# The rotary part of an attention's scores taken over 128 instead of 64 partitions

## The chip, the cores and the metric

The kernel runs on one core of a Trainium2 chip. The metric is the device time of one execution in microseconds (us). Five engines matter: TensorE (PE; its weight loads are listed apart as PEld), VectorE (DVE), ScalarE (ACT), GpSimd (POOL) and the queue of SyncE (SP), which issues the loads of weights.

## The reference, cut to what matters

One block of an encoder: a retention branch and a latent attention branch, merged by gates, then an MLP. The change lies in the attention, 16 heads over 256 tokens. Each head's score has two parts, one over 128 channels of its own and one over 64 rotary channels whose key is the same for all heads:

```python
q_nope, q_pe = q[..., :QK_NOPE], _rope(q[..., QK_NOPE:], positions)      # 128 and 64 wide
k_pe = _rope(k_pe.reshape(B, S, 1, QK_ROPE), positions)                  # one for all heads
qf = jnp.concatenate([q_nope, q_pe], axis=-1)
kf = jnp.concatenate([k_nope, jnp.broadcast_to(k_pe, (B, S, MLA_HEADS, QK_ROPE))], axis=-1)
s = jnp.einsum('bqhd,bkhd->bhqk', qi, k) * scale     # masked by chunks, then softmax, then values
```

## The kernel before

All weights are float32 in memory. A weight tile `raw` is loaded by SP, rounded into `hi` by ACT, and the remainder `lo` is made by DVE; a product of two such pairs takes three matmuls (hi*hi, hi*lo, lo*hi), which the helper `mm3` (lines 585 to 589) writes out. The first 128 queries of a head instead go through one plain float32 matmul, recorded by the profile as two passes (16 heads give 32 records).

The attention is written group by group, four heads to a group: `mla_projections` makes the group's queries, keys and values (tiles `lt`, then `q0`, `qs`, `k0`, `ks`; values in `v`), while `mla_attention` of the group before runs between its steps: `mla_scores`, `mla_turn` (transposes into `mt`), `mla_values` (into `my`). The last group runs between the first products of the output matrix (`mo`). This part has no order written out by hand: a scheduler lays the instructions out for each engine when the program is built, from its own estimates, so an edit moves instructions beyond those that it names. The stages before (`gm` and earlier) and the MLP behind have an order written by hand.

In `mla_scores`, a head h takes eight matmul instructions into one PSUM tile `ms`: line 1014 (own channels, plain float32), line 1015 (rotary channels, plain float32), then `mm3` over the own channels and `mm3` over the rotary channels. The rotary queries of two heads lie on top of each other in one tile of 128 partitions (`pe`, and split in `vkp`), even heads on partitions 0 to 63 and odd heads on 64 to 127; the rotary key `kpe` lies there twice, once in each half. A rotary product of a head therefore takes the slice `b` of 64 partitions. The split rotary key is `kps`, a quarter-thousand columns twice in slot 4 of the big tile `vkp` (line 1006), made once by ACT (line 554) and DVE (line 555).

Of the kernel before, what the change touches and what calls it, by code (L numbers as in the profile page):

```python
# [12 lines left out]
F32 = mybir.dt.float32  # L13
# [6 lines left out]
P = 128  # L20
S = 256
# [84 lines left out]
def block_kernel(ctx: ExitStack, tc: tile.TileContext, A):  # L106
    nc = tc.nc
    V, SC, G, PE = nc.vector, nc.scalar, nc.gpsimd, nc.tensor
# [7 lines left out]
    def big(name, dt=F32, shape=(P, KT, S)):  # L116
        return act.tile(list(shape), dt, tag="act16", name=name)
# [31 lines left out]
    def mmps(name):  # L149
        return pmm.tile([P, 512], F32, tag="mm", name=name)  # L150

    def atps(name):
        return pat.tile([P, 512], F32, tag="at", name=name)
# [40 lines left out]
    def lora_pair(src, x, whole=False):  # L194
        hi, lo = weights(src, [P, 2, LT, P])
        ps = mmps(f"lt{uid[0]}")
        for i in range(2):
            out = ps[:, i * S : (i + 1) * S]
            for k in range(LT):
                PE.matmul(out, hi[:, i, k], x.hi(k), start=k == 0, stop=False)  # L200
                PE.matmul(out, hi[:, i, k], x.lo(k), start=False, stop=False)
            for k in range(LT):
                PE.matmul(out, lo[:, i, k], x.hi(k), start=False, stop=k == LT - 1)
            yield i, out if not whole else ps

    def n_unit(outs, src, x, k0, nk, start, stop):
        for kh in range(0, nk, 2):
            w = weights(src[:, kh : kh + 2], [P, 2, 512])
            first, last = start and kh == 0, stop and kh == nk - 2
            for t, out in enumerate(outs):  # L210
                n_tile(out, w, x, t, k0 + kh, 2, first, last)
# [340 lines left out]
    def split(hi, lo, val, scale=None):  # L552
        if scale is None:
            SC.copy(hi, val)  # L554
            V.tensor_tensor(out=lo, in0=val, in1=hi.bitcast(F32), op=ALU.subtract)  # L555
        else:
            SC.activation(hi, val, AF.Copy, scale=scale)
            V.scalar_tensor_tensor(
                lo, in0=val, scalar=scale, in1=hi.bitcast(F32), op0=ALU.mult, op1=ALU.subtract
            )  # L560
# [24 lines left out]
    def mm3(out, st, mv, start=True, stop=True):  # L585
        (sh, sl), (mh, ml) = st, mv
        PE.matmul(out, sh, mh, start=start, stop=False)
        PE.matmul(out, sh, ml, start=False, stop=False)
        PE.matmul(out, sl, mh, start=False, stop=stop)
# [99 lines left out]
    def rope(out, ps, cos, sin, step):  # L689
        n = ps.shape[1]  # L690
        tmp = rope_pool.tile([P, n, S], F32, tag="rope", bufs=1, name="rope")
        cos, sin = (t.rearrange("p (o n) -> p o n", o=1) for t in (cos, sin))
        for d in range(0, P, step):
            s = d + step if (d // step) % 2 == 0 else d - step
            V.tensor_tensor(
                out=tmp[d : d + step],
                in0=ps[s : s + step],
                in1=sin[s : s + step].to_broadcast([step, n, S]),
                op=ALU.mult,
            )  # L700
        V.tensor_tensor(out=out, in0=ps, in1=cos.to_broadcast([P, n, S]), op=ALU.mult)
        V.tensor_tensor(out=out, in0=out, in1=tmp, op=ALU.add)
# [210 lines left out]
    with ExitStack() as mctx:  # L913
        cc = big("cc", F32R, shape=(P, 2 * LT, 2, S))
        kpe = rope_pool.tile([P, S], F32, tag="kpe", bufs=1, name="kpe")
# [84 lines left out]
        mp = mctx.enter_context(tc.tile_pool(name="mp", bufs=1))  # L1000
# [2 lines left out]
        heads, probs, outs = {}, {}, {}  # L1003

        vkp = big("vkp", F32R, (P, 8, 512))
        kps = vkp[:, 4].rearrange("p (j n) -> p j n", j=2)
        split(kps[:, 0], kps[:, 1], kpe)

        def mla_scores(h):
            q0, qs, k0, ks = heads.pop(h)  # L1010
            pe0, ps = heads[h // 2, "pe"]
            b = slice(64 * (h % 2), 64 * (h % 2) + 64)
            pS = atps(f"ms{h}")
            PE.matmul(pS[:, :P], q0, k0, start=True, stop=False)
            PE.matmul(pS[:, :P], pe0[b, :P], kpe[b, :P], start=False, stop=True)
            mm3(pS[:, P:384], (qs[:, 0], qs[:, 1]), (ks[:, 0], ks[:, 1]), stop=False)
            mm3(pS[:, P:384], (ps[b, 0], ps[b, 1]), (kps[b, 0], kps[b, 1]), start=False)
            pr = mp.tile([P, 384], F32, tag="pr", bufs=3, name=f"pr{h}")
            mx = mp.tile([P, 32], F32, tag="mx", bufs=4, name=f"mx{h}")[:, :4]
            parts = (slice(0, P), slice(P, 384))  # L1020
            for j, sl in enumerate(parts):
                V.tensor_tensor_reduce(
                    pr[:, sl], pS[:, sl], mask[:, sl], QK_SCALE, LOWEST, ALU.add, ALU.max, mx[:, j : j + 1]
                )
            V.tensor_scalar(mx[:, :2], mx[:, :2], -1.0, None, op0=ALU.mult)
            for j, sl in enumerate(parts):
                SC.activation(
                    pr[:, sl], pr[:, sl], AF.Exp, bias=mx[:, j : j + 1],
                    accum_out=mx[:, 2 + j : 3 + j],
                )  # L1030
            V.reciprocal(mx[:, 2:], mx[:, 2:])
            for j, sl in enumerate(parts):
                SC.activation(pr[:, sl], pr[:, sl], AF.Copy, scale=mx[:, 2 + j : 3 + j])
            probs[h] = pr
# [30 lines left out]
        def mla_projections(g):  # L1065
            j0 = 2 * (g % 2)
            for i, ps in lora_pair(A["w_qpe"][g // 2, :, j0 : j0 + 2], cq, True):
                if i:
                    pe = mp.tile([P, 2, S], F32, tag="pe", bufs=2, name=f"pe{g}")
                    rope(pe, ps.rearrange("p (i n) -> p i n", i=2), *tabs[1], 32)  # L1070
                    pes = vkp[:, 5 + g % 2].rearrange("p (i j n) -> p i j n", i=2, j=2)
                    split(pes[:, :, 0], pes[:, :, 1], pe[:, :, P:])
                    for n in range(2):
                        heads[2 * g + n, "pe"] = pe[:, n], pes[:, n]
                yield
            for jj in range(2):
                js = slice(2 * jj, 2 * jj + 2)
                qh = []
                for i, ps in lora_pair(A["w_qn"][g, :, js], cq):
                    h = 4 * g + 2 * jj + i  # L1080
                    q0 = mp.tile([P, P], F32, tag="q0", bufs=6, name=f"q0{h}")
                    qs = mp.tile([P, 2, P], F32R, tag="qs", bufs=6, name=f"qs{h}")
                    SC.copy(q0, ps[:, :P])
                    split(qs[:, 0], qs[:, 1], ps[:, P:])
                    qh.append((q0, qs))
                    yield
                for i, ps in lora_pair(A["w_kn"][g, :, js], ckv):
                    h = 4 * g + 2 * jj + i
                    k0 = mp.tile([P, P], F32, tag="k0", bufs=6, name=f"k0{h}")
                    ks = mp.tile([P, 2, S], F32R, tag="ks", bufs=6, name=f"ks{h}")  # L1090
                    SC.copy(k0, ps[:, :P])
                    split(ks[:, 0], ks[:, 1], ps)
                    heads[h] = (*qh[i], k0, ks)
                    yield
            pss = [mmps(f"v{g}{t}") for t in range(2)]
            for kh in range(2):
                n_unit(pss, A["w_v"][g, :, 2 * kh : 2 * kh + 2], ckv, 2 * kh, 2, kh == 0, kh == 1)
                yield
            vs = vkp[:, 2 * (g % 2) : 2 * (g % 2) + 2]
            split(vs[:, 0], vs[:, 1], pss[0])  # L1100
            v1 = mp.tile([P, 512], F32, tag="v1", bufs=2, name=f"v1{g}")
            SC.copy(v1, pss[1])
            heads[g, "v"] = vs, v1
# [19 lines left out]
        def mla_attention(g):  # L1123
            plan = {}
            slots = SLOTS[g == 3]
            for fn, when in zip((mla_scores, mla_turn, mla_values), slots):
                for i in range(4):
                    plan.setdefault(when[i], []).append((fn, 4 * g + i))
            for slot in range(max(plan) + 1):
                for fn, h in plan.get(slot, ()):  # L1130
                    fn(h)
                yield
# [7 lines left out]
        for g in range(4):  # L1140
            interleave(mla_projections(g), mla_attention(g - 1) if g else iter(()))
# [438 lines left out]
```

## Time and profile before

| | |
|---|---|
| time, median of 3 runs | 1575.42 us (1575.08 to 1575.52) |
| time of the profiled execution | 1575.46 us |
| span of its instructions | 1573.7 us |
| PE busy | 1562.7 us (99%) |
| DVE busy | 1332.8 us (85%) |
| ACT busy | 957.4 us (61%) |
| POOL busy | 36.7 us (2%) |
| granted TensorE clock, mean | 0.998 |

The profiled execution lies within the spread of the timed runs. The 1.8 us between its time and its span lie outside the instructions. The busy time of PE is modelled, and matmuls overlap: a record of 0.28 us can be followed by the next 0.12 us later. The pace is therefore read from the chain of waits, whose pieces do not overlap.

### The profile page before, as it was taken

How to read it: one execution, taken by the hardware profiler on the slowest of the kernel's cores; microseconds unless marked ns; L12 is line 12 of the kernel's file. 1: busy time of each engine (PE TensorE's matmuls, PEld its weight loads, DVE VectorE, ACT ScalarE, POOL GpSimd, SP SyncE). 2: the span in 40 equal slices, each digit the busy share in tenths (PEclk: the TensorE clock that was granted, in tenths of full speed). 3: DMA queues.
4: the chain of work that ended last, by engine and by line, in shares of the span. 5: the costliest groups of instructions: out<-in, count | busy, mean ns of one | idle time of the engine just before them, and what ended most of it. 6: DMA issues, size and time to landing. Idle time of an engine off the chain costs nothing.

```text
span 1573.7 us, 21491 instructions
## 1 busy us (share of the span) xinstructions
PE 1562.7 (99%) x7759; PEld 1319.5 (84%) x7759; DVE 1332.8 (85%) x1775; ACT 957.4 (61%) x1397; POOL 36.7 (2%) x71
## 2 busy tenths in 40 slices
PE   9999999999999999999999999999999999999997
PEld 7888888888898889888888888888888888888886
DVE  7898877899977986764667798999999899979996
ACT  6645655566545656664445576767677766655664
POOL 0000000000000000000000000000000100000000
PEclk9999999999999999999999999999999999999999
DMA  9666655466656563334565676667666977767773
GB/s 321 203 206 205 231 167 162 152 204 207 203 174 225 200 201 135 129 126 147 188 227 175 216 249 213 225 220 228 224 224 210 376 261 244 242 243 255 259 262 116
DMA packets 106986, 332.66 MB, mean 211 GB/s; under 512 B 11136, under 2 KB 12032, under 8 KB 105856
## 3 DMA queue, kind: packets, MB, share of 16 engines
q1 hardware_dynamic: 103632, 317.66, 60.1%
q0 software_dynamic: 3104, 11.54, 1.8%
q10 hardware_dynamic: 144, 2.10, 0.4%
q8 instruction: 61, 1.00, 0.3%
q14 instruction: 45, 0.37, 0.1%
HBM read 318.67 MB, written 12.58 MB: 210 GB/s over the span
## 4 chain that ended last, share of the span: by engine, by line
PE 77%; DVE 3%; issue 1%; ACT 1%; DVEq 0%; POOLq 0%; POOL 0%; ACTq 0%
PE dn L362 7%; PE dn L363 7%; PE dn L361 7%; PE z L176 6%; PE z L180 3%; PE zs L338 3%; PE zs L339 3%; PE zs L337 3%; PE mo L216 2%; PE mo L219 2%; PE mo L217 2%; PE wo L219 2%; PE wo L216 2%; PE wo L217 2%; PE gm L363 2%; PE gm L361 2%
## 5 line engine op out<-in xcount | busy, mean ns | idle before, releaser
L555 DVE TENSOR_TENSOR lo<-raw,hi 128x1024 fp32r<-128x1024 f32 (+3 forms) x238 | 254.4, 1085 | 26.8 <-ACT hi L554 26.4
L554 ACT CAST hi<-raw 128x1024 fp32r<-128x1024 f32 (+3 forms) x238 | 219.2, 940 | 59.1 <-PE yr L363 7.5
L169 DVE TENSOR_TENSOR lo<-raw,hi 128x1024 fp32r<-128x1024 f32 (+1 forms) x148 | 173.3, 1172 | 95.0 <-ACT hi L168 94.8
L168 ACT CAST hi<-raw 128x1024 fp32r<-128x1024 f32 (+1 forms) x148 | 149.5, 1011 | 160.0 <-PE mo L217 47.2
L554 ACT CAST hi<-forms 128x1024 fp32r<-128x1024 f32 x57 | 60.1, 1054 | 75.0 <-DVE forms L311 33.2
L555 DVE TENSOR_TENSOR morelo<-raw,morehi 128x1024 fp32r<-128x1024 f32 (+1 forms) x86 | 91.5, 1084 | 4.0 <-ACT morehi L554 3.9
L361 PE MATMUL dn<-hi,dd 128*128 128x512 f32 x240 | 93.5, 389 | 0.0
L363 PE MATMUL dn<-hi,dd 128*128 128x512 f32 x240 | 93.4, 389 | 0.0
L362 PE MATMUL dn<-lo,dd 128*128 128x512 f32 x240 | 93.4, 389 | 0.0
L554 ACT CAST morehi<-forms 128x1024 fp32r<-128x1024 f32 x51 | 53.8, 1054 | 58.5 <-DVE forms L321 32.1
L554 ACT CAST morehi<-raw 128x1024 fp32r<-128x1024 f32 (+1 forms) x86 | 78.9, 939 | 4.6 <-PE dn L363 2.8
L176 PE MATMUL z<-hT,hi 128*128 128x512 f32 x304 | 75.9, 392 | 0.0
L555 DVE TENSOR_TENSOR lo<-forms,hi 128x1024 fp32r<-128x1024 f32 x57 | 69.6, 1222 | 1.6 <-ACT hi L554 0.4
L311 DVE TENSOR_TENSOR forms<-raw,sraw 128x1024 f32<-128x1024 f32 x54 | 65.9, 1220 | 0.0
L176 PEld LDWEIGHTS z<-hT,hi 128*128 128x128 f32 x304 | 55.7, 188 | 10.7
L555 DVE TENSOR_TENSOR morelo<-forms,morehi 128x1024 fp32r<-128x1024 f32 x51 | 62.3, 1222 | 0.9
L361 PE MATMUL dn<-morehi,dd 128*128 128x512 f32 x146 | 56.8, 389 | 0.0
L362 PE MATMUL dn<-morelo,dd 128*128 128x512 f32 x146 | 56.8, 389 | 0.0
L363 PE MATMUL dn<-morehi,dd 128*128 128x512 f32 x146 | 56.8, 389 | 0.0
L362 PEld LDWEIGHTS dn<-lo,dd 128*128 128x128 f32 x240 | 45.1, 188 | 9.4
L361 PEld LDWEIGHTS dn<-hi,dd 128*128 128x128 f32 x240 | 45.1, 188 | 9.4
L363 PEld LDWEIGHTS dn<-hi,dd 128*128 128x128 f32 x240 | 45.1, 188 | 9.3
(512 smaller groups left out, 4371.2 us busy)
## 6 DMA issues: line engine op xcount, KB each, us to landing
raw<-w_down SPq DMA_DIRECT2D x106, 512.0 KB, 6.0
raw<-w_up SPq DMA_DIRECT2D x64, 512.0 KB, 4.6
raw<-w_rv SPq DMA_DIRECT2D x32, 512.0 KB, 4.6
raw<-w_rg SPq DMA_DIRECT2D x32, 512.0 KB, 4.1
raw<-w_gret SPq DMA_DIRECT2D x32, 512.0 KB, 4.2
raw<-w_ret_o SPq DMA_DIRECT2D x32, 512.0 KB, 4.8
raw<-w_gmla SPq DMA_DIRECT2D x32, 512.0 KB, 4.2
raw<-w_mla_o SPq DMA_DIRECT2D x32, 512.0 KB, 3.5
```

The costliest lines, as they stand in the source:

```text
L168: SC.copy(hi, raw)
L169: V.tensor_tensor(out=lo, in0=raw, in1=hi.bitcast(F32), op=ALU.subtract)
L176: PE.matmul(out, w[0][:, k], x.both(k0 + k), start=start and k == 0, stop=False)
L216: PE.matmul(out, x.hi(k0 + k, ts), w[0][:, k], start=start and k == 0, stop=False)
L217: PE.matmul(out, x.lo(k0 + k, ts), w[0][:, k], start=False, stop=False)
L219: PE.matmul(out, x.hi(k0 + k, ts), w[1][:, k], start=False, stop=stop and k == nk - 1)
L311: V.tensor_tensor(out=self.fa, in0=self.rb[:, 1:].to_broadcast([P, 2, 512]), in1=self.ra, op=ALU.add)
L361: PE.matmul(q, ah, wh, start=start, stop=False)
L362: PE.matmul(q, ah, wl, start=False, stop=False)
L363: PE.matmul(q, al, wh, start=False, stop=self.left[f] == 0)
L554: SC.copy(hi, val)
L555: V.tensor_tensor(out=lo, in0=val, in1=hi.bitcast(F32), op=ALU.subtract)
```

## The change

The rotary key gets a tile `kz` of 128 partitions with two copies: in copy 0 the key stands on partitions 0 to 63 and zeros on the rest, in copy 1 the other way round. POOL clears `kz`, ACT copies `kpe` into its two halves, and the split (ACT and DVE) is now made of `kz`, so it has 512 columns instead of 256 and takes slots 4 and 5 of `vkp`; the split queries move to slots 6 and 7. Each rotary product takes all 128 partitions: the query tile holds two heads, and the zeros of the key's copy remove the other one.

```diff
+        kz = mp.tile([P, 2, S], F32, name="kz")
+        G.memset(kz, 0.0)
+        for i in range(2):
+            b = slice(64 * i, 64 * i + 64)
+            SC.copy(kz[b, i], kpe[b])
-        kps = vkp[:, 4].rearrange("p (j n) -> p j n", j=2)
-        split(kps[:, 0], kps[:, 1], kpe)
+        kps = vkp[:, 4:6].rearrange("p j (i n) -> p j i n", i=2)
+        split(kps[:, 0], kps[:, 1], kz)
...
-            PE.matmul(pS[:, :P], pe0[b, :P], kpe[b, :P], start=False, stop=True)
+            PE.matmul(pS[:, :P], pe0[:, :P], kz[:, i, :P], start=False, stop=True)
...
-            mm3(pS[:, P:384], (ps[b, 0], ps[b, 1]), (kps[b, 0], kps[b, 1]), start=False)
+            mm3(pS[:, P:384], (ps[:, 0], ps[:, 1]), (kps[:, 0, i], kps[:, 1, i]), start=False)
...
-                    pes = vkp[:, 5 + g % 2].rearrange("p (i j n) -> p i j n", i=2, j=2)
+                    pes = vkp[:, 6 + g % 2].rearrange("p (i j n) -> p i j n", i=2, j=2)
```

The number and the columns of the matmuls stay. The scheduler places them anew from head 1 on. Behind line 1007 the line numbers of the changed kernel are 5 higher than those of the kernel before. On PE, around the scores of head 7 (`ms7`), with the transposes of head 4 (`mt4`) and projections of the next group (`lt`) beside them, the kernel before has:

```order
L1040 MATMUL mt4_6027<-con_105,pr4_5892 128x128
L1014 MATMUL ms7_6077<-k07_5797,q07_5741 128x128
L1015 MATMUL ms7_6077<-kpe_4028,pe1_5533 128x128
L1040 MATMUL mt4_6027<-con_105,pr4_5892 128x128 x2
L587 MATMUL ms7_6077<-ks7_5798,qs7_5742 128x256
...
L587 MATMUL ms7_6077<-vkp_5231 128x256
L588 MATMUL ms7_6077<-vkp_5231 128x256
...
L589 MATMUL ms7_6077<-vkp_5231 128x256
```

and the changed kernel, from the float32 product of the rotary channels on:

```order
L1020 MATMUL ms7_6081<-kz_5232,pe1_5537 128x128
...
L587 MATMUL ms7_6081<-ks7_5802,qs7_5746 128x256
L588 MATMUL ms7_6081<-ks7_5802,qs7_5746 128x256
L589 MATMUL ms7_6081<-ks7_5802,qs7_5746 128x256
L587 MATMUL ms7_6081<-vkp_5231 128x256
L588 MATMUL ms7_6081<-vkp_5231 128x256
L589 MATMUL ms7_6081<-vkp_5231 128x256
```

What stood between the rows of head 7's `mm3` over the rotary channels now stands ahead of them. On ACT, at the start of the attention, where the first projections are rounded and copied out (`hi641` is the last weight tile that it rounds ahead of them, `q00` and `k00` belong to head 0), the kernel before has:

```order
L168 CAST hi641_5401<-raw640_5400 128x1024
L1083 COPY q00_5296<-lt633_5283 128x128
L554 CAST qs0_5297<-lt633_5283 128x128
L1091 COPY k00_5337<-lt636_5324 128x128
L554 CAST ks0_5338<-lt636_5324 128x256
L554 CAST vkp_5231<-pe0_5267 128x2x128
L168 CAST hi644_5444<-raw643_5443 128x1024
```

and the changed kernel:

```order
L168 CAST hi641_5405<-raw640_5404 128x1024
L1010 COPY kz_5232<-kpe_4028 64x256 x2
L1088 COPY q00_5300<-lt633_5287 128x128
L554 CAST qs0_5301<-lt633_5287 128x128
L554 CAST vkp_5231<-kz_5232 128x512
L1096 COPY k00_5341<-lt636_5328 128x128
L554 CAST ks0_5342<-lt636_5328 128x256
L554 CAST vkp_5231<-pe0_5271 128x2x128
L168 CAST hi644_5448<-raw643_5447 128x1024
```

Three instructions of ACT have come between; the split of `kpe` has left its old place in the gate stage before. DVE makes the remainder of the split at the same place of its own order:

```order
L555 TENSOR_TENSOR qs0_5301<-lt633_5287,qs0_5301 128x128
L555 TENSOR_TENSOR vkp_5231<-kz_5232,vkp_5231 128x512
L555 TENSOR_TENSOR ks0_5342<-lt636_5328,ks0_5342 128x256
L702 TENSOR_TENSOR pe0_5271<-pe0_5271,rope_5272 128x512
L555 TENSOR_TENSOR vkp_5231<-pe0_5271,vkp_5231 128x2x128
L169 TENSOR_TENSOR lo645_5449<-raw643_5447,hi644_5448 128x1024
L555 TENSOR_TENSOR qs1_5318<-lt633_5287,qs1_5318 128x128
```

In the kernel before the same rows stand without the second. POOL has one new instruction, the clearing, which waits for the last gated output `gm` of the stage before (line 738), since `kz` lies in memory that this stage used. SP's order is the same in both kernels.

## Rows read from the trace of the kernel before

**Rows 1.** Busy us and count by engine in three stretches.

```profile
core 0: us, PE busy (x) PEld busy (x) DVE busy (x) ACT busy (x) POOL busy (x), PEclk, DMA share, GB/s
595.00:700.00 105.00, 105.00 (x710) 94.04 (x709) 73.62 (x171) 72.69 (x201) 0.00 (x0) 1.00 0.39 130
...
910.00:1570.00 660.00, 654.74 (x3129) 549.42 (x3127) 617.77 (x726) 440.16 (x595) 28.34 (x52) 1.00 0.70 239
```

**Rows 2.** Chain of waits over head 3's scores: start us, us, what.

```profile
617.39 0.22 PE ms L1014 x2
617.61 0.41 PE ms L1015 x2
618.03 0.31 PE ms L587
618.34 0.12 PE ms L588
...
618.58 0.31 PE ms L587
618.89 0.12 PE ms L588
...
619.12 0.32 PE lt L200
619.44 0.12 PE lt L201
```

**Rows 3.** Chain of waits, two pieces of head 7's scores.

```profile
649.37 0.12 PE ms L587
...
653.19 0.31 PE ms L589
```

**Rows 4.** Timeline behind head 3: start us, us, engine, line, operation, tiles, shape.

```profile
619.05 0.39 PE L200 MATMUL lt<-cc,hi 128*128 128x256 f32 x1
...
619.16 0.19 PEld L201 LDWEIGHTS lt<-cc,hi 128*128 128x128 f32 x1
```

**Rows 5.** Timeline of ACT at the start of the attention.

```profile
587.17 1.03 ACT L168 CAST hi<-raw 128x1024 fp32r<-128x1024 f32 x1
588.69 0.27 ACT L1083 COPY q<-lt 128x128 f32<-128x128 f32 x1 [0.49 <-PE lt L203]
...
593.01 0.41 ACT L554 CAST vkp<-pe 128x256 fp32r<-128x256 f32 x1 [2.39 <-DVE pe L702]
594.18 1.05 ACT L168 CAST hi<-raw 128x1024 fp32r<-128x1024 f32 x1 [0.77 <-PE lt L201]
```

**Rows 6.** Timeline of DVE in the same stretch.

```profile
584.02 1.88 DVE L738 TENSOR_TENSOR gm<-gm,kcsums 128x512 f32<-128x512 f32 x3
...
592.29 0.68 DVE L702 TENSOR_TENSOR pe<-pe,rope 128x512 f32<-128x512 f32 x1
...
596.40 0.48 DVE L555 TENSOR_TENSOR qs<-lt,qs 128x128 fp32r<-128x128 f32 x2
```

**Rows 7.** Tile vkp, splits of 512 columns: durations ns min/median/max.

```profile
L554 ACT CAST vkp<-v x4: 582/588/589, 603.0 to 691.8; 128x512 fp32r<-128x512 f32 x4
L555 DVE TENSOR_TENSOR vkp<-v,vkp x4: 691/692/692, 603.6 to 692.4; 128x512 fp32r<-128x512 f32 x4
```

**Rows 8.** POOL's two clearings of float32: busy us, mean ns.

```profile
L563 POOL MEMSET ones<- 128x128 f32 x1 | 0.2, 204 | 0.3 <-POOLq L1570 0.3
...
L565 POOL MEMSET negh<- 128x2 f32 x1 | 0.1, 99 | 0.0
```

**Rows 9.** Timeline of PE, head 0's first rotary product and the values' first product.

```profile
595.94 0.49 PE L1015 MATMUL ms<-kpe,pe 64*128 64x128 f32 x2
...
597.45 0.50 PE L216 MATMUL v<-hi,cc 128*128 128x512 f32 x1
```

**Rows 10.** Timeline, DVE's queries of heads 9 and 10 and PE's next product.

```profile
655.24 0.48 DVE L555 TENSOR_TENSOR qs<-lt,qs 128x128 fp32r<-128x128 f32 x2
...
655.91 0.48 PE L216 MATMUL v<-hi,cc 128*128 128x512 f32 x1
```

More of the change, by code (lines that the diff above doesn't have):

```diff
@@ L1011, in mla_scores @@
             pe0, ps = heads[h // 2, "pe"]
-            b = slice(64 * (h % 2), 64 * (h % 2) + 64)
+            i = h % 2
             pS = atps(f"ms{h}")
             PE.matmul(pS[:, :P], q0, k0, start=True, stop=False)
-            PE.matmul(pS[:, :P], pe0[b, :P], kpe[b, :P], start=False, stop=True)
+            PE.matmul(pS[:, :P], pe0[:, :P], kz[:, i, :P], start=False, stop=True)
             mm3(pS[:, P:384], (qs[:, 0], qs[:, 1]), (ks[:, 0], ks[:, 1]), stop=False)
-            mm3(pS[:, P:384], (ps[b, 0], ps[b, 1]), (kps[b, 0], kps[b, 1]), start=False)
+            mm3(pS[:, P:384], (ps[:, 0], ps[:, 1]), (kps[:, 0, i], kps[:, 1, i]), start=False)
             pr = mp.tile([P, 384], F32, tag="pr", bufs=3, name=f"pr{h}")
```

## The prediction

> **What bounds the kernel now.** I first read the stretches with each engine's busy time. In the attention PE is busy for all of its 105 us, at a granted clock of 1.00 (the 2.4 GHz level), while DVE and ACT are busy for 74 and 73 of them [rows 1]. So PE sets the pace here, and a microsecond off its path is worth a microsecond as long as the other two keep up. Busy time does not tell how well the time is used, because records overlap; for that I read the chain of waits, piece by piece. The reader should look there at the same instruction in different company. A product of 256 columns normally takes 0.12 us, whether on all 128 partitions (line 588 at 618.34) or on 64 (line 588 at 618.89) [rows 2]. Line 587 of a head's own channels takes 0.12 us behind a product of 128 partitions [rows 3] but 0.31 us behind the rotary product of line 1015, and line 587 of the rotary channels takes 0.31 us again; the projection behind the block takes 0.32 us, its successor 0.12 [rows 2]. The two float32 passes of line 1014 take 0.22 us, those of line 1015, of the same width, 0.41 [rows 2]. The extra time stands where the partitions change from 128 to 64 or back, and nowhere else. The row that carries it can belong to any line and any tile.
>
> The Trainium skill, "TensorEngine Tiling (Array Packing)", Key Properties, says that a change between whole and partial array makes TensorE drain first, while moving from one partial tile to another does not. The trace agrees and adds the price that the page lacks.
>
> **What the change removes.** Entering costs 0.41 - 0.22 = 0.19 or 0.31 - 0.12 = 0.19 us; leaving costs 0.31 - 0.12 = 0.19 or 0.32 - 0.12 = 0.20 us [rows 2, 3]. Fifteen heads have two rotary blocks each (line 1015, and `mm3` over `vkp`), with work on 128 partitions before and behind. Head 7 has three, because the order of before puts the last product of its `mm3` behind a projection, and that product indeed takes 0.31 us alone at 653.19 [rows 3]. That makes 33 blocks: 33 x 0.19 + 33 x 0.195 = 6.27 + 6.44 = 12.7 us. With every product on 128 partitions all of it goes.
>
> **What it adds on PE.** Nothing: the same count of products with the same columns. That a whole-array product costs no more than a half-array one is the 0.12 against 0.12 and the second pass of line 1015, which must fit in 0.41 - 0.19 = 0.22 us for two, as in line 1014 [rows 2].
>
> **What it adds elsewhere.** POOL clears 512 columns. Its cost is not in the trace; from 99 ns for 2 columns and 204 for 128 [rows 8] a straight line gives 0.1 + 510 x 0.105 / 126 = 0.52 us, and the ends are 0.20 us (the row of 128 columns) and four times that, 0.82 us. It may start when the last gated output is done, 584.02 + 1.88 = 585.90 [rows 6], so `kz` is clear by 586.1 to 586.8. ACT reaches its two copies at 587.17 + 1.03 = 588.20 [rows 5]; the clearing makes nobody wait, at either end.
>
> The copies are 64 partitions by 256 columns, a shape that no row has. Between 0.27 us (128 columns) and 0.41 us (256 columns) each [rows 5], I take 0.35: ACT is done by 588.9 instead of standing idle until 588.69, so `q00` comes 0.0 to 0.3 us late. The 512-column rounding (0.59 us [rows 7]) follows `q00` and `qs0` and ends about 590.0, where in the trace ACT waited for PE again. DVE's remainder of 0.69 us [rows 7] stands ahead of line 702, which moves from 592.29 to 592.98 and ends at 593.66 instead of 592.97 [rows 6]. Two things wait behind it. Head 0's first rotary product starts at 595.94 [rows 9]: 2.3 us are left. ACT's split of `pe` moves from 593.01 to 593.7 and ends at 594.1, just before PE frees the buffer for the next rounding at 594.18 [rows 5]. So this cover holds, with 0.1 us to spare on ACT. Were it gone, the `hi` at 594.18, the `lo` behind it, `qs` and finally the first product of `v` would be late by as much: at most 0.7 us, once. The old split of `kpe` in the gate stage was off the path and its going gives nothing.
>
> **What is late next.** Work released by PE keeps its distance from PE, since both come earlier. What can become late is work that does not start earlier. At the first values product PE arrives at 597.45 [rows 9] less four changes, 0.77 us, that is 596.68; DVE's first `qs` of the pair, half of the row of 0.48 us, is done at 596.40 + 0.28 (a single one's length) = 596.68 [rows 6]. That hand-off comes out at zero, give or take 0.3 us. The other near one is at 655.91, where the pair of `qs` ends at 655.72 [rows 10]; head 7's six changes lie in front of it, 1.2 us, but in the new order head 7's scores stand together and the transposes of head 4 ahead of them, and DVE makes the weights' remainder before head 7's maxima. I cost this at 0.1, with 0 and 1.0 as ends (all of the 1.2 less the 0.2 spare). Altogether I take 0.4 us of new waits, with ends 0 and 2.
>
> The stages behind keep their order and SP's queue. In the MLP DVE is busy for 618 of 660 us and PE idles for 5 [rows 1], but that stage starts when its inputs are made by PE, so it moves as a whole.
>
> **Sum.** 1575.46 (the profiled execution, 0.04 above the median) - 12.7 + 0.4 = 1563.2, taken as 1563.1 us against the median.
>
> **Rivals.**
>
> 1. *New waits eat a part.* The scheduler has moved softmax, transposes and value splits against each other from head 1 on, from its own estimates. ACT and DVE have 30 of 105 us free [rows 1], which speaks against more than a few short waits; that two hand-offs are within 0.4 us speaks for some. With one wait of 0.7 us at each of the three group boundaries and the 0.4 above: 1575.4 - 12.7 + 2.5 = 1565.2 us; it ends near 1569, half of the gain.
>
> 2. *A weight load that no longer hides (slower).* If on the whole array a weight load had to wait for the matmul in flight, each of the five rotary loads of a head (two passes, three products) would show its 0.19 us [rows 4]: 16 x 5 x 0.19 = 15.2, and 1575.4 - 12.7 + 15.2 = 1577.9 us. It would outweigh the gain from 67 exposed loads on. Against it: behind head 3 a load on 128 partitions starts at 619.16, while the product that began at 619.05 and lasts 0.39 us is running on the same 128 partitions [rows 4], and such products follow each other at 0.12 us [rows 2]. The Trainium skill, "TensorE: Matmul & The Clock Gate", Part 3 (Packing small matmuls), speaks for this rival: loads run ahead of a matmul in flight only if they address other rows of the array. By that rule the sum would be 1577.9; this trace contradicts it for whole-array loads.
>
> 3. *The gap stays.* If the extra time hung on the tiles (a float32 product beside rounded ones, a first use of `vkp`) and not on the partitions, the time would be 1575.4 us. Against it: it also falls on projections and on head 7's single product, and not on line 587 at 649.37 [rows 2, 3]. Should only the float32 blocks (line 1015) be mended, half would remain: 1569 us.
>
> **Chances.** Forecast (waits up to 1 us) 0.75; rival 1 beyond that 0.17; half of the gaps remain 0.03; no change 0.03; slower 0.02. About 0.2% (3 us) is what a measurement of this kernel can tell from no change. Only "the gap stays" lies within it, so faster 0.95, same 0.03, slower 0.02. The range: at the low end no new wait and changes of 0.20 us, 66 x 0.20 = 13.2, gives 1562.2, and a little below for the measurement, 1561.8; at the high end rival 1 with twice its waits, 1567.0.
>
> **What would show it.** In the changed profile no matmul of the attention has 64 partitions; lines 1020 and 587 to 589 stand in the chain at 0.22 and 0.12 us, and the product behind a block at its ordinary pace. Head 0's scores start at about 595.9 as before, and the last product of the attention comes 12 to 13 us earlier than now. Waits of PE for `kz`, for `qs` or for a transposed softmax would show rival 1; pieces of 0.3 us at rotary products on 128 partitions would show rival 2. I am wrong if the time is above 1567 us.

## The result and the profile after

The changed kernel takes 1563.11 us (median of 4 runs, 1562.88 to 1563.40) against 1575.25 us (1574.23 to 1575.52) of the kernel before on the same chip: a ratio of 0.9924, 95% interval 0.9907 to 0.9941. It is 12.1 us faster; 1563.1 was predicted. The profiled execution took 1563.23 us, its instructions span 1561.4 us.

First, where in the program the time went: the first products of `wo` (behind the attention) and the last group of `dn` (end of the MLP), durations ns min/median/max, first and last start us. In the kernel before:

```profile
L216 PE MATMUL wo<-hi,mg x128: 389/389/478, 800.1 to 890.0; 128*128 128x512 f32 x128
L363 PE MATMUL dn<-hi,dd x240: 389/389/397, 1232.0 to 1563.2; 128*128 128x512 f32 x120
```

and in the changed one:

```profile
L216 PE MATMUL wo<-hi,mg x128: 389/389/478, 787.8 to 877.7; 128*128 128x512 f32 x128
L363 PE MATMUL dn<-hi,dd x240: 389/389/397, 1219.7 to 1550.9; 128*128 128x512 f32 x120
```

`wo` starts 12.3 us earlier, and the last `dn` comes 763.1 us behind it in both: all was gained ahead of `wo`. Before the attention the two executions are 0.36 us apart; from the end of the last gate product to the end of the first `wo` product before takes 216.29 us and after 204.36, so the attention gave 11.93 us.

The table of stretches (busy us and count by engine) answers to [rows 1]; the second stretch is taken 12.3 us earlier, where the same part of the MLP lies:

```profile
core 0: us, PE busy (x) PEld busy (x) DVE busy (x) ACT busy (x) POOL busy (x), PEclk, DMA share, GB/s
595.00:700.00 105.00, 104.89 (x763) 98.83 (x762) 77.91 (x186) 77.34 (x212) 0.00 (x0) 1.00 0.43 142
897.70:1557.70 660.00, 654.84 (x3129) 549.33 (x3127) 617.59 (x726) 440.15 (x595) 28.43 (x52) 1.00 0.69 239
```

PE is as busy as before, at the same granted clock; what changed is that 763 matmuls pass in the 105 us instead of 710. The MLP stretch holds the same count of instructions of every engine and the same busy times within 0.2 us. The chain of waits over one head's scores answers to [rows 2] (start us, us, what):

```profile
614.86 0.22 PE ms L1019 x2
615.09 0.22 PE ms L1020 x2
615.31 0.12 PE ms L587
...
615.67 0.12 PE ms L587
...
616.02 0.12 PE lt L200
```

The four pieces that had 0.41, 0.31, 0.31 and 0.32 us in [rows 2] have 0.22, 0.12, 0.12 and 0.12. The weight loads show how. At head 0's rotary `mm3` of before (PEld: start us, us, line):

```profile
596.59 0.19 PEld L589 LDWEIGHTS ms<-ks,qs 128*128 128x128 f32 x1
596.90 0.18 PEld L587 LDWEIGHTS ms<-vkp 64*128 64x128 f32 x1
...
597.13 0.19 PEld L589 LDWEIGHTS ms<-vkp 64*128 64x128 f32 x1
597.45 0.19 PEld L216 LDWEIGHTS v<-hi,cc 128*128 128x128 f32 x1
```

and of the changed kernel:

```profile
595.84 0.19 PEld L589 LDWEIGHTS ms<-ks,qs 128*128 128x128 f32 x1
595.96 0.19 PEld L587 LDWEIGHTS ms<-vkp 128*128 128x128 f32 x1
596.09 0.19 PEld L588 LDWEIGHTS ms<-vkp 128*128 128x128 f32 x1
```

Ordinary loads follow each other at 0.11 to 0.13 us, each running beside the matmuls ahead of it. At a change, in either direction, the load comes later: the first one for 64 partitions starts 0.31 us behind its predecessor, the first one for 128 partitions behind the block 0.32 us. It is not made ahead. That the price of a change (0.19 us) is the length of a load fits this; the last section has the changes where the load is shorter.

What prepares the zero-padded key (tile `kz`, ns min/median/max and start):

```profile
L1010 ACT COPY kz<-kpe x2: 400/401/402, 587.7 to 588.2; 64x256 f32<-64x256 f32 x2
L1007 POOL MEMSET kz<- x1: 527/527/527, 585.7 to 585.7; 128x512 f32 x1
L554 ACT CAST vkp<-kz x1: 623/623/623, 589.0 to 589.0; 128x512 fp32r<-128x512 f32 x1
L555 DVE TENSOR_TENSOR vkp<-kz,vkp x1: 681/681/681, 591.6 to 591.6; 128x512 fp32r<-128x512 f32 x1
```

What is behind it on ACT, answering to [rows 5], and PE's two products that could have been late, answering to [rows 9]:

```profile
593.25 0.41 ACT L554 CAST vkp<-pe 128x256 fp32r<-128x256 f32 x1 [2.99 <-DVE pe L702]
593.77 1.05 ACT L168 CAST hi<-raw 128x1024 fp32r<-128x1024 f32 x1
...
595.50 0.39 PE L1020 MATMUL ms<-kz,pe 128*128 128x128 f32 x2
...
596.43 0.40 PE L216 MATMUL v<-hi,cc 128*128 128x512 f32 x1
```

None of the PE rows names an idle time in front of it. One new wait did appear, where the second group of values begins (chain of waits):

```profile
619.80 0.88 ACT pr L1032 x4
620.67 0.15 ACT q L1088
620.82 0.17 ACT qs L554
...
621.01 0.30 DVE qs L555
...
621.36 0.50 PE v L216
```

The chain leaves PE here: the product of line 216 takes 0.61 us from the end of the matmul before it, instead of 0.23, because the split queries (`qs`) come late; ACT had four pieces of softmax ahead of the copies they need. In the kernel before the same product (624.63) came 1.20 us after its `qs`.

**The account.** I took, for every matmul between 585 and 745 us of the kernel before, the time from the end of its predecessor to its own. The 33 entries into 64 partitions together show 6.34 us more than ordinary, the 33 exits 6.35: 12.69 us. Of this 0.38 goes to the new wait and 0.10 to the 48 rounded rotary products, which take 0.119 instead of 0.117 us on average; that leaves 12.21. The 0.28 us that are missing to 11.93 are spread thinly over the other products (the 480 `lt` products together take 0.12 us more), and no row names a cause. Another execution of the changed kernel (experiment 7) has the same attention within 0.04 us.

### The profile page after: what moved, and what is told of

It reads as the page before. It is cut to its first block, busy times and chain, and to the rows that moved or that the text cites. A ratio compares the mean times of both kernels' runs of the same rounds, so it can differ in the third digit from the quotient of the medians.

```text
span 1561.4 us, 21494 instructions
## 1 busy us (share of the span) xinstructions
PE 1549.9 (99%) x7759; PEld 1314.9 (84%) x7759; DVE 1332.3 (85%) x1775; ACT 957.7 (61%) x1399; POOL 37.3 (2%) x72
## 4 chain that ended last, share of the span: by engine, by line
PE 79%; DVE 1%; issue 1%; ACT 1%; DVEq 0%; POOLq 0%; POOL 0%; ACTq 0%
PE dn L361 7%; PE dn L363 7%; PE dn L362 7%; PE z L176 7%; PE z L180 3%; PE zs L338 3%; PE zs L337 3%; PE zs L339 3%; PE mo L216 2%; PE mo L217 2%; PE mo L219 2%; PE wo L216 2%; PE wo L217 2%; PE wo L219 2%; PE yr L363 2%; PE yr L362 2%
```

## Experiments

All ran beside the kernel before, which took 1575.03 to 1575.09 us (medians on three chips). "Changes" counts the passages of PE between 128 and 64 partitions, either way, in the attention.

**1. The padded key with the old slices.** Everything of the change stays (clearing, copies, the 512-column split, `kz`), only the products take 64 partitions again. 68 changes (66 in the kernel before).

```
+            b = slice(64 * i, 64 * i + 64)
-            PE.matmul(pS[:, :P], pe0[:, :P], kz[:, i, :P], ...)
+            PE.matmul(pS[:, :P], pe0[b, :P], kz[b, i, :P], ...)
...
-            mm3(..., (ps[:, 0], ps[:, 1]), (kps[:, 0, i], kps[:, 1, i]), ...)
+            mm3(..., (ps[b, 0], ps[b, 1]), (kps[b, 0, i], kps[b, 1, i]), ...)
```

> The changed kernel with its cleared tile, its copies and its 512-column split kept, but every rotary product taken over 64 partitions again (the half of kz and of its split that holds the key). Its PE order has 68 changes between 64 and 128 partitions (66 in the kernel before, none in the changed one). Theory (each change of partitions costs 0.19 us, nothing else does): 1562.7 + 68 x 0.1925 = 1575.8 us, and 0.31 us pieces at line 587 again. Rival (the gain came from another layout of the key, or from the scheduler's new order): 1563 to 1566 us. Rival (preparing kz costs something that the changed kernel hides): above 1577 us.

Measured 1575.77 us (1575.05 to 1576.39), ratio 1.0003 [0.9994, 1.0013]. The gain goes with the partitions alone; the new tile costs nothing that can be told. Its chain has the old prices:

```profile
614.19 0.41 PE ms L1021 x2
614.61 0.31 PE ms L587
...
615.16 0.31 PE ms L587
```

**2. Only the float32 product whole.** The slice `b` stays in the `mm3` line alone. 36 changes.

```
             PE.matmul(pS[:, :P], pe0[:, :P], kz[:, i, :P], ...)
-            mm3(..., (ps[:, 0], ps[:, 1]), (kps[:, 0, i], kps[:, 1, i]), ...)
+            mm3(..., (ps[b, 0], ps[b, 1]), (kps[b, 0, i], kps[b, 1, i]), ...)
```

> The changed kernel with only the float32 rotary product over 128 partitions; the three rounded products over 64. 36 changes in its PE order, 48 half-array products. Theory: 1562.7 + 36 x 0.1925 = 1569.6 us, the float32 piece at 0.22, line 587 of the rotary channels at 0.31. Rival (the cost hangs on the float32 product, whose type differs from its neighbours): 1563 us. Rival (the cost is one per half-array product, 12.7 us over 64): 1562.7 + 48 x 0.2 = 1572.2 us.

Measured 1569.44 us (1569.14 to 1569.97), ratio 0.9965 [0.9952, 0.9977].

```profile
616.29 0.22 PE ms L1021 x2
616.51 0.12 PE ms L587
...
616.86 0.31 PE ms L587
```

**3. Only the `mm3` whole.** The other half of the change. 32 changes.

```
-            PE.matmul(pS[:, :P], pe0[:, :P], kz[:, i, :P], ...)
+            PE.matmul(pS[:, :P], pe0[b, :P], kz[b, i, :P], ...)
             mm3(..., (ps[:, 0], ps[:, 1]), (kps[:, 0, i], kps[:, 1, i]), ...)
```

> The mirror image: only the three rounded rotary products over 128 partitions, the float32 one over 64. 32 changes, 16 half-array products. Theory: 1562.7 + 32 x 0.1925 = 1568.9 us. Rival (float32 alone carries the cost): 1575 us. Rival (a cost per half-array product): 1562.7 + 16 x 0.2 = 1565.9 us.

Measured 1568.99 us (1568.78 to 1569.19), ratio 0.9961 [0.9946, 0.9976].

```profile
616.03 0.41 PE ms L1021 x2
616.45 0.31 PE ms L587
...
617.00 0.12 PE ms L587
```

In 2 and 3 the gap stays at the block that was left on 64 partitions, and each block carries its half. So it belongs neither to the mixture of float32 and rounded products nor to a tile.

**4. The kernel before with its blocks side by side.** No zeros, no new tile: every rotary product keeps its 64 partitions, but a head's rotary `mm3` is written ahead of the `mm3` over its own channels, so that the two blocks touch. 42 changes.

```
-            mm3(..., (qs[:, 0], qs[:, 1]), (ks[:, 0], ks[:, 1]), stop=False)
-            mm3(..., (ps[b, 0], ps[b, 1]), (kps[b, 0], kps[b, 1]), start=False)
+            mm3(..., (ps[b, 0], ps[b, 1]), (kps[b, 0], kps[b, 1]), stop=False)
+            mm3(..., (qs[:, 0], qs[:, 1]), (ks[:, 0], ks[:, 1]), start=False)
```

> The kernel before with one edit: the three rounded rotary products are written ahead of the three own-channel products of the head, so that they stand right behind the float32 rotary product. All 64 products of before stay on 64 partitions, no kz; 42 changes instead of 66. Theory (the change of partitions costs, not the half-array product): 1562.7 + 42 x 0.1925 = 1570.8 us. Rival (a cost per half-array product): 1575.4 us, unchanged.

Measured 1570.78 us (1570.28 to 1571.03), ratio 0.9972 [0.9961, 0.9983].

```profile
616.21 0.41 PE ms L1015 x2
616.63 0.12 PE ms L587
...
616.98 0.32 PE ms L587
```

This one separates changes from half-array work: experiment 1 has as many rotary products on 64 partitions as this one, and 26 more changes. One line goes through all four: 1562.7 us (the changed kernel less its wait) and 0.1925 us for each change gives 1575.8, 1569.6, 1568.9 and 1570.8; measured were 1575.77, 1569.44, 1568.99 and 1570.78.

**5. Two heads at a time.** If a change is the price, fewer changes can be had by taking two heads together, the even on the lower and the odd on the upper partitions. The kernel before, its rotary products alternating between the halves; the scheduler pulled three of the eight pairs apart, and 26 changes remained.

```
...
+            for p, b in zip(pS, bs):                       # pS, bs: two heads' tiles and halves
+                PE.matmul(p[:, :P], pe0[b, :P], kpe[b, :P], start=False, stop=True)
+            for n, (i, j) in enumerate(((0, 0), (0, 1), (1, 0))):
+                for p, b in zip(pS, bs):
+                    PE.matmul(p[:, P:384], ps[b, i], kps[b, j], start=n == 0, stop=False)
...
```

> The kernel before (all 64 rotary products on 64 partitions, no kz) with the products of two heads written together: own float32 products, then the rotary products of both heads in turn (even head on partitions 0 to 63, odd head on 64 to 127), then the own rounded products. 26 changes between 64 and 128 partitions instead of 66. For seven of the eight pairs the two halves alternate, product by product. Theory (only changes between half and whole cost; a change from one half to the other is free and halves run one after the other): 1562.7 + 26 x 0.1925 = 1567.7 us, plus up to 1 us of waits since two score tiles are held at once. Rival A (products in opposite halves run at the same time): the float32 passes and rounded products of seven pairs, 7 x (4 x 0.11 + 6 x 0.12) = 8.1 us, shrink to half: 1563.7 us, with pieces near zero in the chain. Rival B (a change from half to half costs the same as half to whole): nine further changes in each alternating pair (12 rounded and float32 starts less the first), 7 x 7 x 0.19 = 9 us more: 1577 us.

Measured 1564.66 us (1564.51 to 1564.94), ratio 0.9934 [0.9919, 0.9949]. The line through experiments 1 to 4 gives 1567.7 for 26 changes: my theory of changes alone missed by 3.0 us, and the rival that the two halves run at the same time is within 1.0. Its pieces near zero are in the trace: neighbours on opposite halves end 3 to 25 ns apart. That a half product costs as much as a whole one [rows 2] is thus true only where its neighbours lie on the same half.

**6. The zeros made a stage earlier.** `kz` in a buffer that is free before, cleared and filled in the gate stage, to see whether its preparation cost anything.

```
+        kz = rope_pool.tile([P, 2, S], F32, tag="val", bufs=2, name="kz")
+        G.memset(kz, 0.0)                                  # at the start of the gate stage
...
+            for i in range(2):                             # right behind the key's rotation
+                SC.copy(kz[64 * i : 64 * i + 64, i], kpe[64 * i : 64 * i + 64])
```

> The changed kernel with kz in memory that is free long before the attention: POOL clears it early and ACT copies the key into it in the stage before; the split too moves out of the attention's start. Everything is on 128 partitions, no change of partitions. Theory (preparing kz at the start of the attention is hidden): the same time as the changed kernel within 0.4 us (the one wait of 0.38 us on PE that the changed kernel shows can go or stay with the scheduler's order): 1562.7 to 1563.3 us. Rival (the preparation delays PE's first scores): 1 us or more below the changed kernel.

Measured 1562.49 us (1562.34 to 1562.90), ratio 0.9920 [0.9907, 0.9934]. Its attention takes 203.97 us against 204.36 of the changed kernel and 204.32 of its repeat (7). The difference, 0.35 to 0.39, is the size of the one wait, and that wait is gone here: the scheduler put the query copies elsewhere, and the pair of `qs` is made in time (DVE, then PE):

```profile
620.03 0.48 DVE L555 TENSOR_TENSOR qs<-lt,qs 128x128 fp32r<-128x128 f32 x2
...
620.91 0.48 PE L216 MATMUL v<-hi,cc 128*128 128x512 f32 x1
```

No rest is left for the preparation, so it was hidden in the changed kernel. As the order moved with it, this shows no more than that.

**7. The changed kernel again,** on the chip of 5 and 6.

> The changed kernel once more, beside the others on the same chip: 1563.1 us, and one piece of about 0.6 instead of 0.23 us in PE's chain at the second group's first values product.

Measured 1563.11 us (1562.90 to 1563.45), ratio 0.9924 [0.9912, 0.9937]; the wait is there again (621.65, 0.61 us from end to end), so it belongs to the order and not to one execution.

**8. Pairs kept together.** Experiment 5 with the rotary products of a pair held in their written order and ahead of other work. All 8 pairs stand whole, 16 changes.

```
...
+            with tc.high_priority():
+                for p, b in zip(pS, bs):
+                    tc.keep_in_program_order(PE.matmul(p[:, :P], pe0[b, :P], kpe[b, :P], ...))
+                for n, (i, j) in enumerate(((0, 0), (0, 1), (1, 0))):
+                    for p, b in zip(pS, bs):
+                        tc.keep_in_program_order(PE.matmul(p[:, P:384], ps[b, i], kps[b, j], ...))
```

> The two-head kernel of before (half-array products, even and odd head in turn) with the scheduler held to that order: the rotary products of each of the eight pairs stand together, alternating halves, 16 changes of partitions. Theory after the run of the two-head kernel (a change of half and whole costs 0.19 us each; neighbours in opposite halves run at the same time, 6 to 10 ns apart): a pair's rotary block took 0.78 us from the end before it to its last end there, and 0.32 to the end of the next product; on the whole array ten pieces of 0.11 to 0.12 and one of 0.12 make 1.28, so 8 x 0.18 = 1.5 us below a kernel without changes (1562.7): 1561.2 us, up to 0.5 more for waits. Rival (no concurrency, only fewer changes): 1562.7 + 16 x 0.1925 = 1565.8 us.

Measured 1562.25 us (1561.85 to 1562.37), ratio 0.9918 [0.9905, 0.9932]. The chain over one pair:

```profile
613.39 0.42 PE ms L1021 x4
613.81 0.35 PE ms L1025 x6
614.16 0.32 PE ms L587
```

Ten products take 0.42 + 0.35 = 0.77 us, of which 0.19 is the entry: 0.58, while on the whole array they take 4 x 0.111 + 6 x 0.119 = 1.16. Neighbours on opposite halves end 2 to 11 ns apart, over all eight pairs. With both changes a pair takes 0.77 + 0.32 = 1.09 us, on the whole array 1.16 + 0.12 = 1.28: 8 x 0.19 = 1.5 us less than 1562.7, or 1561.2. The rest is one wait of the first values product (PE):

```profile
596.62 0.50 PE L216 MATMUL v<-hi,cc 128*128 128x512 f32 x1 [0.73 <-DVE qs L555]
```

From the end of the product before it to its own it takes 1.231 us instead of 0.231; without that 1.0 us the time would be 1561.25. This version is the fastest by median (0.9 us below the changed kernel, 0.2 below experiment 6), but less than 0.2% from either, and the intervals of the ratios overlap.

**9. The same pairs, one head after the other.** As 8, but the rotary products of the even head all come first, then the odd head's: only in one place do neighbours lie on opposite halves.

```
-                for n, (i, j) in enumerate(((0, 0), (0, 1), (1, 0))):
-                    for p, b in zip(pS, bs):
+                    for n, (i, j) in enumerate(((0, 0), (0, 1), (1, 0))):   # inside the loop over heads
```

> The same kernel with one edit: within a pair, all rotary products of the even head come first, then all of the odd head, so neighbours lie in the same half, but for the one place where the heads meet. 16 changes as in the alternating kernel, the same 64 half-array products. Theory (only neighbours in opposite halves overlap): 1565.8 us less one overlap of 0.11 us in each pair, 0.9: 1564.9 us. Rival (what helped in the two-head kernel was the lower number of changes or the longer block, not the alternation): the same time as the alternating kernel.

Measured 1563.77 us (1563.68 to 1564.70), ratio 0.9930 [0.9917, 0.9944], with the same 1.0 us wait at the values. Halves that can run together only as neighbours would have given 1564.9; that missed by 1.1 us, or 2.1 without the wait. The chain over the same pair:

```profile
613.27 0.52 PE ms L1021 x3
613.79 0.01 PE ms L1024
613.80 0.10 PE ms L1021
613.90 0.35 PE ms L1024 x5
614.25 0.32 PE ms L587
```

In the program two passes of line 1021 and three products of line 1024 (even head) come first, then the same of the odd head. In the trace the odd head's passes have only one product of line 1024 ahead of them: the first of them starts at 613.417 and ends at 613.791, while at least two of the even head's three products, which stand before it in the program, end at 613.921 or later. Starts and modelled ends a few ns apart would not carry this alone; the length of the block does. In the order of the program, with the one overlap where the heads meet, it would take 0.19 + 1.16 - 0.11 = 1.24 us; it takes 0.98, 0.79 without its entry (alternating 0.58), and nearly the same in all eight pairs. PE has taken work for the free half from further back. Against the alternating kernel that is 8 x 0.21 = 1.7 us more; measured were 1.5.

## Why the prediction was right

- **What bounds.** PE's path set the attention, and the gap stands at the change of partitions: shown by 1 to 4, where nothing but the number of changes orders the times. The 105 us of [rows 1] are only a stretch of the attention, which is 216 us long; but from 585 to 790 us of the trace of before, too, no product that follows its like on 128 partitions takes over 0.06 us more than its ordinary pace.
- **What is removed.** 33 blocks at 0.19 + 0.195, 12.7 us, against 12.69 in the account.
- **What PE adds.** "Nothing" was near: 0.10 us over the 48 rounded rotary products. It is no price of the whole array either: line 589 of the own channels, on 128 partitions in both kernels, went from 0.115 to 0.118 us as well.
- **What the preparation adds.** The clearing took 0.527 us (0.52 taken, ends 0.20 and 0.82), the copies 0.40 each (0.35 taken; near the upper end of 0.41), the rounding 0.623 (0.59), DVE's remainder 0.681 (0.69). ACT's split of `pe` came at 593.25 and the next rounding at 593.77 with no idle time between that waits for it; the cover that was put at 0.1 us held.
- **New waits.** The sum came out (0.4 taken, 0.38 measured), the place did not, so the agreement in size is luck, and with it the last tenths of 1563.1 against 1563.11: the two hand-offs that the prediction named did not wait, and a third did. At the first values product `qs` ended 0.15 us before PE came (the first of a pair that starts at 596.00, 0.28 us long, so 596.28, against 596.43; "zero, give or take 0.3 us"). The one at 655.91 [rows 10], named as the other near one, did not wait: in the changed kernel that pair of `qs` ends at 648.90 and the product starts at 649.89. PE waited at an earlier group boundary (621.36), which had 1.20 us of slack in the trace of before. I ranked hand-offs by their slack in the old order, but the scheduler had moved four pieces of softmax ahead of the query copies, which the old slack cannot show. That this order and not the shift in time makes the wait is supported by 6, which has the same products and another order, and no wait; it was not tried by itself.
- **What is behind.** The MLP moved as a whole: 763.1 us from `wo` to the last `dn`, before and after.
- **The rivals.** A weight load that no longer hides: loads on the whole array start 0.11 to 0.13 us apart, as above. The Trainium skill, "TensorE: Matmul & The Clock Gate", Part 3 (Packing small matmuls), lets loads run ahead only where they address other rows; by that rule the time would have been 1577.9 us, and the trace after contradicts it. An earlier sentence of the same section of the Trainium skill also lets a load run ahead into a background weight buffer; loads of 0.19 us on the whole array at 0.12 us distance agree with that one. [rows 4], which the prediction took against the rival, was a weak witness: the product recorded at 619.05 begins with its own load of 0.19 us, so the load at 619.16 began beside that load; the next one (619.28) is the first that began while the product itself ran. The gap that stays: 1 to 4. New waits beyond 1 us: one of 0.38. The upper end of the range, 1567.0, is the three waits of 0.7 doubled without the 0.4 beside them; with that doubled too it would be 1567.7, and the result is far below either.
- **From one half to the other.** "The trace agrees" held for the change between whole and part alone: in the kernel before no neighbours lie on opposite halves. That such neighbours pass without the 0.19 us was shown by 5 and 8.

The forecast compared the change with half-array products that stand alone on their half, and for that case the cost of giving up 64 partitions is nothing. It did not ask what those products could do in company; 5, 8 and 9 show that the other half of the array was free to be used.

## What to carry to other kernels

Where PE sets the pace, look in the chain of waits for the same product with two durations, and for what stands ahead of the longer one; count the passages between part and whole array, not the products. They can be avoided by padding with zeros, as here, or by putting partial products of opposite halves together, where they overlap; both ended within 1 us. For new waits, read the new order of the engine that feeds PE: slack in the old order says little once a scheduler has moved the feeder's work.

## What was not expected of the hardware

- Products on opposite halves of the array overlap almost wholly (ends 2 to 11 ns apart in experiment 8, 0.58 us for ten instead of 1.16), and they do so in part when they are not neighbours in the program (0.79). The Trainium skill, "TensorE: Matmul & The Clock Gate", Part 3 (Packing small matmuls), states the first, and that matmuls start in program order; experiment 9 agrees with the one and not with the other.
- The price of a change goes with the length of the weight load behind it, and not with the columns of the product. Transposes (`mt`) have the shorter load in the kernel before (ns min/median/max):

```profile
L1040 PEld LDWEIGHTS mt<-con,pr x48: 138/140/143, 615.4 to 732.6; 128*128 128x128 f32 x48
L1014 PEld LDWEIGHTS ms<-k,q x32: 186/192/192, 591.2 to 714.6; 128*128 128x128 f32 x32
```

Both make products of 128 columns, which take 0.11 us each ordinarily. Right behind a rotary block (chain of waits):

```profile
607.82 0.42 PE ms L1014 x2
...
615.49 0.48 PE mt L1040 x3
```

The exit into line 1014 costs 0.42 - 0.22 = 0.20 us, the one into line 1040 0.48 - 0.33 = 0.15. All 302 changes of the kernel before and of experiments 1 to 5, 8 and 9 fit, each taken against the ordinary pace of its kind of product: 0.190 to 0.196 us behind loads of 0.182 or 0.183 (entries), 0.194 to 0.204 behind loads of 0.186 or 0.187, and 0.148 to 0.151 behind the seven of 0.138 or 0.139. No experiment varied the load alone, so this is a fit and not a test.
